# Transposing the experts' activations: TensorE with an identity, or VectorE in blocks of 32 with the blocks exchanged by the loads

## The chip, the cores and the metric

The kernel runs on one core of one Trainium2 chip. The metric is the time of one execution on the device in microseconds (us); lower is better. Three executions of the kernel before took 3319.48 to 3320.54 us, with a median of 3319.95 us.

## The reference, cut to what matters

The model is two transformer-like blocks over 256 tokens of width 2048. The change lies wholly in the last part of the first block, a retrieval over 16,384 experts of one neuron each:

```python
def peer_ffn(h, w_q, sub_keys, u, v):
    ...
    s1, i1 = lax.top_k(scores[:, :, 0], PEER_TOPK)        # 16 of 128 first keys
    s2, i2 = lax.top_k(scores[:, :, 1], PEER_TOPK)        # 16 of 128 second keys
    ...
    cand_idx = i1 * PEER_N_KEYS + i2                      # expert = 128 * first key + second key
    top_scores, top_pos = lax.top_k(cand_scores, PEER_TOPK)
    gates = jax.nn.softmax(top_scores, axis=-1)
    ...
        a = jnp.einsum('td,thkd->thk', xb, u[eb])
        w = gb * jax.nn.gelu(a, approximate=False)
        return jnp.einsum('thk,thkd->td', w, v[eb])
```

The kernel does not gather rows of u and v. It computes gelu(x u^T) for all 16,384 experts as a dense product, multiplies it by a table of gates that is zero wherever a token did not choose an expert, and multiplies the result by v as a second dense product.

## The kernel before

All dense products have one form. `jobs` is a list of 1 MB weight blocks in the order in which they are used; `load` fetches each block into a `raw` tile from SyncE's queue, four blocks ahead. `convert` cuts a block into four pieces of 128x512, and `split` makes of each piece a `hi` part (ScalarE, L208) and a `lo` part (VectorE, L209), so that TensorE works at its fast number format with three matmuls for each 128x512 piece and token block (`passes`, L260, L261, L263). With two token blocks a piece is six matmuls and a job is 24. VectorE and ScalarE prepare up to `PIECES = 7` pieces ahead of TensorE, in eight `hi` and eight `lo` buffers. Work that is not a dense product is put into `tasks`, whose steps are woven in between the pieces: `tasks.step()` runs once for each piece and issues one step for each lane. Every engine runs its instructions in the order in which the program issues them.

The experts' part has two phases:

- The in phase, `expert_in_jobs(g)` for g = 0 to 31: four jobs for each group of 512 experts (four first keys times 128 second keys). At the end of a group `post` applies the gelu on ScalarE (L936) and leaves `ga`, with tokens on partitions and experts along the row. The second product needs experts on partitions. So `work` has TensorE transpose the eight 128x128 blocks against the identity (`transposed`, L230), ScalarE copies the results out of PSUM into `aT` (L942), and GpSimd's queue stores `aT` in device memory as `ad` (L944). This work starts four steps after the group ends.
- The out phase, `expert_out_jobs(pair)` for 16 pairs of groups: eight jobs for each pair. While one pair is multiplied, the next is prepared: before the pair's first and second job `weights_load` issues the loads of one group each, one load of `ad` (L952) and four loads of the gate table (L954), all on GpSimd's queue; before the fourth and the sixth job `weigh` multiplies activations and gates on VectorE (L963) and splits the product into `h` and `l` with one ScalarE and one VectorE instruction of 128x1024 (L208, L209). These are what TensorE loads as weights in the next pair.

During the first half of the in phase VectorE also does the routing (`top`, `route`), and GpSimd scatters the gates into the tables `gd` with 256 indirect DMAs (L914). There is one table for each 64 tokens (`QT = 64`), with second keys along partitions, then first keys, then tokens. SyncE's queue clears the tables beforehand with 16 transfers (L926).

Of the kernel before, what the change touches and what calls it, by code (L numbers as in the profile page):

```python
# [17 lines left out]
F32 = mybir.dt.float32  # L18
# [5 lines left out]
OP = mybir.AluOpType  # L24
AX = mybir.AxisListType

P, T, D, TB = 128, 256, 2048, 2
NEG = -1.0e30
PACE = 3.7
QT = 64  # L30
# [80 lines left out]
def hybrid_block_kernel(ctx: ExitStack, tc: tile.TileContext, a: dict, out: bass.AP):  # L111
    nc = tc.nc
    V, A, G, PE = nc.vector, nc.scalar, nc.gpsimd, nc.tensor
# [9 lines left out]
    dram = ctx.enter_context(tc.tile_pool(name="dram", bufs=1, space=bass.MemoryType.DRAM))  # L123
# [4 lines left out]
    def nm(s):  # L128
        count[0] += 1
        return f"{s}_{count[0]}"  # L130

    def s4(shape, dt=F32):
        return s4p.tile([P] + shape, dt, tag="s4", name=nm("s4"))

    def s2(shape, dt=F32):
        return s2p.tile([P] + shape, dt, tag="s2", name=nm("s2"))

    def small(n):
        t = smp.tile([P, 32], F32, tag="sm", name=nm("sm"))
        return t[:, 0:n]  # L140

    def kept(shape, dt=F32, name="kept", p=P):

        if name in SHARED:
            return const.tile([p] + shape, dt, name=nm(name), tag=SHARED[name], bufs=2)
        return const.tile([p] + shape, dt, name=nm(name))
# [4 lines left out]
    def side():  # L151
        return sidep.tile([P, 512], F32, tag="side", name=nm("side"))
# [53 lines left out]
    def split(hi, lo, src):  # L206

        A.copy(out=hi, in_=src)  # L208
        V.tensor_tensor(out=lo, in0=src, in1=hi.bitcast(F32), op=OP.subtract)  # L209
# [13 lines left out]
    def transposed(src_of, n):  # L223

        for c in range(0, n, 2):
            pt = side()
            pv = pt.rearrange("p (c t) -> p c t", c=2)
            for i in range(min(2, n - c)):
                for tb in range(TB):
                    PE.transpose(pv[:, i, tb * P:(tb + 1) * P], src_of(c + i, tb), ident)  # L230
            yield pv, c
# [17 lines left out]
    tasks = Tasks(4, 4)  # L249
# [53 lines left out]
    S = {}  # L303
# [459 lines left out]
    fox_group(3)  # L763
    out_jobs("f", 1)
    jobs[-4].pre = lambda: S.update(clear_t=tasks.add(clear_tables(), apart=8, lane=1))
    mla_group(3)
    gate_jobs("m", 2)
# [32 lines left out]
    def rf(tb):  # L800
        return S["rf"][:, tb:tb + 1]
# [19 lines left out]
    def peer_q_jobs():  # L821
# [5 lines left out]
        for b in range(4):  # L827
            def post(ps, b=b):
# [32 lines left out]
                for tb in range(TB):  # L861
                    ts = [tasks.add(top(tb, hh), [t], 1, 2) for hh in range(2)]
                    rs.append(tasks.add(route(tb, b), ts, 1, 2))
                S["gates_t"].append(tasks.add(scatter(b), rs + [S["clear_t"]], 1, 3))
            block_jobs([a["wpq"][b, k] for k in range(4)], post, pre=peer_pace if b == 0 else None)

    def route(tb, b):

        hs = slice(2 * b, 2 * b + 2)
        tv, tp, ti = S["tv"][tb][:, hs], S["tp"][tb][:, hs], S["ti"][tb][:, :, hs]  # L870
        pick = S["pick"][tb]
        gp = s2([2, 2, 16])
        gate, place = gp[:, 0], gp[:, 1]
        ab = s2([2, 2, 16], U32)
        V.tensor_tensor(out=gate, in0=tv, in1=tv[:, :, 0:1].to_broadcast([P, 2, 16]), op=OP.subtract)
        V.tensor_scalar(out=ab[:, 0], in0=tp, scalar1=4, scalar2=None, op0=OP.logical_shift_right)
        V.tensor_scalar(out=ab[:, 1], in0=tp, scalar1=15, scalar2=None, op0=OP.bitwise_and)
        A.activation(out=gate, in_=gate, func=AF.Exp)
        abf, ie = s2([2, 2, 16]), s2([2, 2, 16])
        V.tensor_copy(out=abf, in_=ab)  # L880
        yield
        sm, rs = small(2), small(2)
        V.tensor_reduce(out=sm, in_=gate, axis=AX.X, op=OP.add)
        V.reciprocal(out=rs, in_=sm)
        V.tensor_tensor(out=gate, in0=gate, in1=rs[:, :, None].to_broadcast([P, 2, 16]), op=OP.mult)
        for i in range(2):
            eq = s2([2, 16, 16])
            V.tensor_tensor(out=eq, in0=abf[:, i][:, :, :, None].to_broadcast([P, 2, 16, 16]),
                            in1=S["iota"][:, None, None, 0:16].to_broadcast([P, 2, 16, 16]), op=OP.is_equal)
            V.tensor_tensor(out=eq, in0=eq, in1=ti[:, i][:, :, None, :].to_broadcast([P, 2, 16, 16]), op=OP.mult)  # L890
            V.tensor_reduce(out=ie[:, i], in_=eq, axis=AX.X, op=OP.add)
            yield
        V.scalar_tensor_tensor(out=abf[:, 0], in0=ie[:, 0], scalar=float(QT),
                               in1=S["lane"][:, None, :].to_broadcast([P, 2, 16]), op0=OP.mult, op1=OP.add)
        V.scalar_tensor_tensor(out=place, in0=ie[:, 1], scalar=float(P * QT), in1=abf[:, 0], op0=OP.mult, op1=OP.add)
        for to in range(2):
            for half in range(2):
                dst = pick[half * QT:(half + 1) * QT, to, :, hs]
                rows, ks = slice(to * QT, (to + 1) * QT), slice(8 * half, 8 * half + 8)
                V.tensor_copy(out=dst[:, 0], in_=gate[rows, :, ks])  # L900
                V.tensor_copy(out=dst[:, 1].bitcast(U32), in_=place[rows, :, ks])
        yield END

    def scatter(b):

        for h in (2 * b, 2 * b + 1):  # L910
            for k in range(8):
                for q, gd in enumerate(S["gd"]):
                    pick = S["pick"][q // 2][:, q % 2]
                    G.indirect_dma_start(  # L914
                        out=gd.rearrange("p (n o) -> (p n) o", o=1),
                        out_offset=bass.IndirectOffsetOnAxis(ap=pick[:, 1, h, k:k + 1].bitcast(U32), axis=0),
                        in_=pick[:, 0, h, k:k + 1], in_offset=None, compute_op=OP.add)
                yield
        yield END

    def clear_tables():

        S["gd"] = [dram.tile([P, P * QT], F32, name=f"gd{q}") for q in range(T // QT)]
        for i in range(4):
            for gd in S["gd"]:
                nc.sync.dma_start(out=gd[:, i * 2048:(i + 1) * 2048].rearrange("p (a b) -> p a b", a=8),  # L926
                                  in_=warm.bitcast(F32)[:, None, :].to_broadcast([P, 8, 256]))
                yield
        yield END

    def expert_in_jobs(g):

        def post(ps):
            ga = s4([TB, 512])
            for tb in range(TB):
                A.activation(out=ga[:, tb], in_=ps[tb], func=AF.Gelu, scale=rf(tb))  # L936
            aT = s4([4, T])
            S["ad", g] = dram.tile([P, 4 * T], F32, name=f"ad{g}")

            def work():  # L940
                for pv, c in transposed(lambda c, tb: ga[:, tb, c * P:(c + 1) * P], 4):
                    A.copy(out=aT[:, c:c + 2, :], in_=pv)  # L942
                yield
                G.dma_start(out=S["ad", g], in_=aT.rearrange("p j t -> p (j t)"))  # L944
                yield END
            tasks.add(work())
        block_jobs([a["ut"][g, k] for k in range(4)], post)

    def weights_load(g):
        tasks.flush(S["gates_t"])  # L950
        aT, gg = s4([4, T]), s4([T // QT, 4, QT])
        G.dma_start(out=aT.rearrange("p j t -> p (j t)"), in_=S["ad", g])  # L952
        for q, gd in enumerate(S["gd"]):
            G.dma_start(out=gg[:, q].rearrange("p j t -> p (j t)"), in_=gd[:, g * 4 * QT:(g + 1) * 4 * QT])  # L954
        S["loaded", g] = (aT, gg)

    def weigh(g):

        def work():
            aT, gg = S["loaded", g]  # L960
            h, l = s4([4, T], F32R), s4([4, T], F32R)
            av = aT.rearrange("p j (c t) -> p c j t", t=QT)
            V.tensor_tensor(out=av, in0=av, in1=gg, op=OP.mult)  # L963
            split(h, l, aT)
            S["W", g] = (h, l)
            yield END
        S["W_t", g] = tasks.add(work(), (), 1, 1)
# [33 lines left out]
    def peer_start():  # L1001
        iota, lane = kept([16], name="iota"), kept([16], name="lane")
        for dst, step, mul in ((iota, 1, 0), (lane, 0, 1)):
            G.iota(dst, pattern=[[step, 16]], base=0, channel_multiplier=mul,
                   allow_small_or_imprecise_dtypes=True)
        V.tensor_scalar(out=lane[QT:P], in0=lane[QT:P], scalar1=-float(QT), scalar2=None, op0=OP.add)
        S["iota"], S["lane"] = iota, lane

    for g in range(32):
# [590 lines left out]
```

## Time and profile before

| what | value |
|---|---|
| median of three executions | 3319.95 us (3319.48 to 3320.54) |
| profiled execution: its own time | 3319.21 us |
| profiled execution: span of the trace | 3317.4 us |
| TensorE busy in the span | 3288.9 us (99%) |
| VectorE busy | 2324.9 us (70%) |
| ScalarE busy | 1779.5 us (54%) |
| GpSimd busy | 559.3 us (17%) |
| TensorE's granted clock, mean | 0.997 |
| device memory, mean | 204 GB/s |

The span is what the profiler saw from the first to the last instruction; 1.8 us of the execution's own time lie around it. Busy times of an engine count overlapping instructions once. A matmul's duration in the trace is longer than its distance to the next one, because matmuls are pipelined; what a matmul costs is read from the starts.

### The profile page before, as it was taken

How to read it: one execution, taken by the hardware profiler on the slowest of the kernel's cores; microseconds unless marked ns; L12 is line 12 of the kernel's file. 1: busy time of each engine (PE TensorE's matmuls, PEld its weight loads, DVE VectorE, ACT ScalarE, POOL GpSimd, SP SyncE). 2: the span in 40 equal slices, each digit the busy share in tenths (PEclk: the TensorE clock that was granted, in tenths of full speed). 3: DMA queues.
4: the chain of work that ended last, by engine and by line, in shares of the span. 5: the costliest groups of instructions: out<-in, count | busy, mean ns of one | idle time of the engine just before them, and what ended most of it. 6: DMA issues, size and time to landing. Idle time of an engine off the chain costs nothing.

```text
span 3317.4 us, 43290 instructions
## 1 busy us (share of the span) xinstructions
PE 3288.9 (99%) x15275; PEld 2734.3 (82%) x15276; DVE 2324.9 (70%) x4667; ACT 1779.5 (54%) x3125; POOL 559.3 (17%) x494
## 2 busy tenths in 40 slices
PE   9999999999999999999999999999999999999997
PEld 7888888888888888888888888888888888788886
DVE  6677676776677787444566767767668777778767
ACT  6655555554655655555554444444555454455553
POOL 0000000000008777876111111100000000000001
PEclk9999999999999999999999999999999999999999
DMA  6444555688457777777676666665564445444554
GB/s 244 172 159 159 178 178 184 210 267 272 178 184 208 205 215 208 207 216 205 235 278 242 243 249 235 239 235 211 200 224 168 167 170 199 177 165 165 178 190 140
DMA packets 158362, 676.55 MB, mean 204 GB/s; under 512 B 50465, under 2 KB 67249, under 8 KB 86593
## 3 DMA queue, kind: packets, MB, share of 16 engines
q1 hardware_dynamic: 102416, 613.06, 52.6%
q0 software_dynamic: 55296, 60.45, 7.6%
q8 instruction: 119, 1.95, 0.2%
q14 instruction: 99, 0.80, 0.1%
q10 hardware_dynamic: 432, 0.29, 0.0%
HBM read 635.58 MB, written 38.15 MB: 203 GB/s over the span
## 4 chain that ended last, share of the span: by engine, by line
PE 98%; DVE 2%; issue 0%; ACT 0%; DMA 0%; DVEq 0%; SPq 0%
PE acc L263 30%; PE acc L260 30%; PE acc L261 30%; PE side L230 3%; PE side L576 2%; PE side L542 1%; PE side L552 0%; PE side L553 0%; PE side L551 0%; DVE lo L209 0%; DVE X L1318 0%; PE side L839 0%; DMA X<-in_x_dram 0%; DVE X L1323 0%; DVE lst L1304 0%
## 5 line engine op out<-in xcount | busy, mean ns | idle before, releaser
L209 DVE TENSOR_TENSOR lo<-raw,hi 128x512 fp32r<-128x512 f32 x2244 | 1506.1, 689 | 784.3 <-ACT hi L208 775.9
L208 ACT CAST hi<-raw 128x512 fp32r<-128x512 f32 x2244 | 1369.8, 622 | 1128.7 <-DVE lo L209 610.4
L260 PE MATMUL acc<-hi,xh 128*128 128x512 f32 x2816 | 1122.7, 399 | 2.0 <-ACT xh L1352 0.9
L263 PE MATMUL acc<-hi,xl 128*128 128x512 f32 x2816 | 1098.9, 391 | 2.8 <-DVE xl L209 2.8
L261 PE MATMUL acc<-lo,xh 128*128 128x512 f32 x2816 | 1098.4, 390 | 3.0 <-DVE lo L209 3.0
L260 PE MATMUL acc<-hi,s 128*128 128x512 f32 x1664 | 654.5, 393 | 0.0
L261 PE MATMUL acc<-lo,s 128*128 128x512 f32 x1664 | 647.6, 389 | 0.0
L263 PE MATMUL acc<-hi,s 128*128 128x512 f32 x1664 | 646.1, 389 | 0.0
L263 PEld LDWEIGHTS acc<-hi,xl 128*128 128x128 f32 x2816 | 529.5, 188 | 116.0 <-DVE xl L209 4.1
L261 PEld LDWEIGHTS acc<-lo,xh 128*128 128x128 f32 x2816 | 530.2, 188 | 108.3 <-DVE lo L209 4.6
L260 PEld LDWEIGHTS acc<-hi,xh 128*128 128x128 f32 x2816 | 530.2, 188 | 107.7 <-ACT xh L1352 1.6
L914 POOL DMA_INDIRECT gd<-pick x256 | 426.2, 1665 | 89.6 <-issue 73.6
L263 PEld LDWEIGHTS acc<-hi,s 128*128 128x128 f32 x1664 | 312.4, 188 | 65.4
L261 PEld LDWEIGHTS acc<-lo,s 128*128 128x128 f32 x1664 | 312.6, 188 | 63.3
L260 PEld LDWEIGHTS acc<-hi,s 128*128 128x128 f32 x1664 | 312.6, 188 | 63.1
L1329 POOL TENSOR_TENSOR X<-X,s 128x512 f32<-128x512 f32 x6 | 9.0, 1524 | 874.4 <-ACT X L1328 874.4
L535 ACT ACTIVATE s<-s,sm 128x128 f32<-128x128 f32 (+1 forms) x128 | 57.3, 448 | 123.4 <-DVE sm L533 123.4
L1217 DVE SCALAR_TENSOR_TENSOR s<-s,vec,s 128x256 f32<-128x256 f32 x240 | 115.6, 482 | 4.6
L952 POOL DMA_DIRECT2D s<-ad x32 | 17.1, 534 | 483.1 <-PE acc L263 447.7
L944 POOL DMA_DIRECT2D ad<-s x32 | 26.9, 839 | 406.8 <-ACT s L942 406.8
L230 PEld LDWEIGHTS side<-cst,s 128*128 128x128 f32 x720 | 84.1, 141 | 11.1
L230 PE MATMUL side<-cst,s 128*128 128x128 f32 x720 | 92.6, 272 | 0.0
(257 smaller groups left out, 1699.9 us busy)
## 6 DMA issues: line engine op xcount, KB each, us to landing
raw<-in_ut_dram SPq DMA_DIRECT2D x128, 1024.0 KB, 4.9
raw<-in_pv_dram SPq DMA_DIRECT2D x128, 1024.0 KB, 5.3
raw<-in_w_dram SPq DMA_DIRECT2D x120, 1024.0 KB, 4.8
raw<-in_win_dram SPq DMA_DIRECT2D x87, 1024.0 KB, 5.0
raw<-in_wout_dram SPq DMA_DIRECT2D x32, 1024.0 KB, 5.7
raw<-in_wo_dram SPq DMA_DIRECT2D x32, 1024.0 KB, 4.7
gd<-s SPq DMA_DIRECT2D x16, 1024.0 KB, 9.1
raw<-in_wpq_dram SPq DMA_DIRECT2D x16, 1024.0 KB, 4.7
```

What stands on the lines that cost most here:

```text
L208: A.copy(out=hi, in_=src)
L209: V.tensor_tensor(out=lo, in0=src, in1=hi.bitcast(F32), op=OP.subtract)
L230: PE.transpose(pv[:, i, tb * P:(tb + 1) * P], src_of(c + i, tb), ident)
L260: PE.matmul(ps[tb], lhsT=lh[:, kc, t], rhs=wh, start=start, stop=False)
L261: PE.matmul(ps[tb], lhsT=lh[:, kc, t], rhs=wl, start=False, stop=False)
L263: PE.matmul(ps[tb], lhsT=ll[:, kc, t], rhs=wh, start=False, stop=stop)
L535: A.activation(out=pr[:, c], in_=pr[:, c], func=AF.Exp, bias=nmax[:, i:i + 1], accum_out=sums[:, i:i + 1])
L542: PE.transpose(pt[:, i * P:(i + 1) * P], pr[:, i * P:(i + 1) * P], ident)
L576: PE.matmul(sc[:, o0:o0 + k1], lhsT=q[:, q0:q0 + P], rhs=k[:, 0:k1], start=i == 0, stop=i == len(parts) - 1)
L914: G.indirect_dma_start(out=gd.rearrange("p (n o) -> (p n) o", o=1), out_offset=bass.IndirectOffsetOnAxis(ap=pick[:, 1, h, k:k + 1].bitcast ...
L944: G.dma_start(out=S["ad", g], in_=aT.rearrange("p j t -> p (j t)"))
L1217: V.scalar_tensor_tensor(out=cv[:, c], in0=pad[:, k:k + T], scalar=tapw(k), in1=cv[:, c], op0=OP.mult, op1=OP.add)
```

## The change

The transposes by TensorE and the copies out of PSUM go. VectorE transposes `ga` instead, with one instruction for each token block (128x512), which turns each 32x32 block by itself and leaves the blocks where they are among the partitions. `ad` is stored in that form. The loads put the blocks in place: four loads of `ad`, each into 32 partitions, fetch runs of 512 bytes (128 elements) from all 128 rows. What arrives has tokens in another order along the row (token block, 32 tokens, first key, token), so the gate tables are given the same order: `gd` gets a dimension for the two halves of 64 tokens, the scatter's positions change, and each load of a gate table fetches two runs of 512 bytes for each partition where it fetched one of 1 KB. `weigh` writes `h` and `l` back in the old order, through a rearranged view. The task starts one step after the group ends and goes on at each step, where it waited four.

```diff
-        V.scalar_tensor_tensor(out=abf[:, 0], in0=ie[:, 0], scalar=float(QT),
+        V.scalar_tensor_tensor(out=abf[:, 0], in0=ie[:, 0], scalar=32.0,
...
                     G.indirect_dma_start(
-                        out=gd.rearrange("p (n o) -> (p n) o", o=1),
+                        out=gd.rearrange("p i (n o) -> (p i n) o", o=1),
...
-        S["gd"] = [dram.tile([P, P * QT], F32, name=f"gd{q}") for q in range(T // QT)]
+        S["gd"] = [dram.tile([P, 2, P * 32], F32, name=f"gd{q}") for q in range(T // QT)]
...
-                nc.sync.dma_start(out=gd[:, i * 2048:(i + 1) * 2048].rearrange("p (a b) -> p a b", a=8),
+                nc.sync.dma_start(out=gd[:, i // 2, i % 2 * 2048:(i % 2 + 1) * 2048].rearrange("p (a b) -> p a b", a=8),
...
             for tb in range(TB):
                 A.activation(out=ga[:, tb], in_=ps[tb], func=AF.Gelu, scale=rf(tb))
-            aT = s4([4, T])
-            S["ad", g] = dram.tile([P, 4 * T], F32, name=f"ad{g}")
+            gt = s4([TB, 4, 4, 32])
+            S["ad", g] = dram.tile([P, TB, 4, P], F32, name=f"ad{g}")
 
             def work():
-                for pv, c in transposed(lambda c, tb: ga[:, tb, c * P:(c + 1) * P], 4):
-                    A.copy(out=aT[:, c:c + 2, :], in_=pv)
-                yield
-                G.dma_start(out=S["ad", g], in_=aT.rearrange("p j t -> p (j t)"))
+                for tb in range(TB):
+                    V.transpose(out=gt[:, tb].rearrange("p q b c -> p b q c"), in_=ga[:, tb])
+                    yield
+                G.dma_start(out=S["ad", g], in_=gt.rearrange("p t q b c -> p t q (b c)"))
                 yield END
-            tasks.add(work())
+            tasks.add(work(), (), 1)
...
-        aT, gg = s4([4, T]), s4([T // QT, 4, QT])
-        G.dma_start(out=aT.rearrange("p j t -> p (j t)"), in_=S["ad", g])
+        aT, gg = s4([TB, 4, 4 * 32]), s4([T // QT, 2, 4 * 32])
+        for q in range(4):
+            G.dma_start(out=aT[32 * q:32 * q + 32],
+                        in_=S["ad", g][:, :, q].rearrange("(i r) t x -> r t i x", i=4))
         for q, gd in enumerate(S["gd"]):
-            G.dma_start(out=gg[:, q].rearrange("p j t -> p (j t)"), in_=gd[:, g * 4 * QT:(g + 1) * 4 * QT])
+            G.dma_start(out=gg[:, q], in_=gd[:, :, g * 4 * 32:(g + 1) * 4 * 32])
...
-            av = aT.rearrange("p j (c t) -> p c j t", t=QT)
-            V.tensor_tensor(out=av, in0=av, in1=gg, op=OP.mult)
-            split(h, l, aT)
+            av = aT.rearrange("p t i x -> p (t i x)")
+            V.tensor_tensor(out=av, in0=av, in1=gg.rearrange("p q i x -> p (q i x)"), op=OP.mult)
+            hv, lv = (x.rearrange("p b (g c) -> p g b c", c=32) for x in (h, l))
+            split(hv, lv, aT.rearrange("p t i (b c) -> p (t i) b c", b=4))
...
-        V.tensor_scalar(out=lane[QT:P], in0=lane[QT:P], scalar1=-float(QT), scalar2=None, op0=OP.add)
+        for i in range(1, 4):
+            rows = slice(32 * i, 32 * i + 32)
+            V.tensor_scalar(out=lane[rows], in0=lane[rows], scalar1=float(P * 32 * (i % 2) - 32 * i), scalar2=None,
+                            op0=OP.add)
```

## Rows read from the trace of the kernel before

**Rows 1.** The page, part 1: busy us (share of the span), instructions.

```profile
PE   3288.9 (99%) x15275; PEld 2734.3 (82%) x15276; DVE 2324.9 (70%) x4667; ACT 1779.5 (54%) x3125; POOL 559.3 (17%) x494
```

**Rows 2.** The waits of TensorE, whole span: us in total, times, longest.

```profile
PE acc L261 <- DVE lo L209: 3.0, 2, 2.8
...
PE acc L260 <- ACT hi L208: 0.3, 1, 0.3
```

**Rows 3.** Timeline of TensorE, one group of the in phase: start, us, instruction.

```profile
1315.41 1.04 PE L230 MATMUL side<-cst,s 128*128 128x128 f32 x8
1316.21 0.48 PE L260 MATMUL acc<-hi,xh 128*128 128x512 f32 x1
1316.52 0.40 PE L261 MATMUL acc<-lo,xh 128*128 128x512 f32 x1
1316.75 0.39 PE L263 MATMUL acc<-hi,xl 128*128 128x512 f32 x1
...
1337.84 0.40 PE L263 MATMUL acc<-hi,xl 128*128 128x512 f32 x1
1338.07 1.03 PE L230 MATMUL side<-cst,s 128*128 128x128 f32 x8
```

**Rows 4.** Line 230 in 960 to 1700 us: ns min/median/max, first and last start.

```profile
L230 PE MATMUL side<-cst,s x256: 272/272/273, 975.5 to 1678.7; 128*128 128x128 f32 x128
```

**Rows 5.** Groups by line and shape, VectorE: busy us, mean ns, idle before.

```profile
L209 DVE TENSOR_TENSOR lo<-raw,hi 128x512 fp32r<-128x512 f32 x2240 | 1504.4, 689 | 784.3 <-ACT hi L208 775.9 <-PE acc L263 2.9
...
L1323 DVE SCALAR_TENSOR_TENSOR X<-X,sm,s 128x512 f32<-128x512 f32 x10 | 8.2, 850 | 0.1
```

**Rows 6.** Timeline of ScalarE at the end of a group.

```profile
1628.08 1.37 ACT L936 ACTIVATE s<-acc,rf 128x512 f32<-128x512 f32 x2
1629.35 0.61 ACT L208 CAST hi<-raw 128x512 fp32r<-128x512 f32 x1
```

**Rows 7.** Stretches of 80 us: length, busy PE, PEld, DVE, ACT, POOL, clock, DMA.

```profile
1055.00:1135.00 80.00, 80.00 (x371) 66.58 (x370) 64.06 (x175) 46.83 (x76) 58.71 (x39) 1.00 0.74 208
...
1760.00:1840.00 80.00, 80.00 (x354) 66.28 (x353) 56.25 (x82) 39.54 (x63) 7.93 (x15) 1.00 0.68 242
```

**Rows 8.** Timeline of GpSimd's queue, the first two groups that are loaded.

```profile
1612.52 0.53 POOL L952 DMA_DIRECT2D s<-ad  x1
1613.04 2.13 POOL L954 DMA_DIRECT2D s<-gd  x4
...
1619.25 0.54 POOL L954 DMA_DIRECT2D s<-gd  x1 [2.49 <-DMA s<-ad]
```

**Rows 9.** Timeline of GpSimd's queue, loads of a pair in the out phase.

```profile
1756.62 0.53 POOL L952 DMA_DIRECT2D s<-ad  x1 [35.44 <-PE acc L263]
...
1762.06 0.53 POOL L952 DMA_DIRECT2D s<-ad  x1 [2.80 <-PE acc L263]
```

**Rows 10.** Timeline of VectorE, where the same pair is weighed.

```profile
1779.61 1.22 DVE L963 TENSOR_TENSOR s<-s,s 128x1024 f32<-128x1024 f32 x1
...
1790.54 1.22 DVE L963 TENSOR_TENSOR s<-s,s 128x1024 f32<-128x1024 f32 x1
```

**Rows 11.** DMA queues, 1740 to 1827 us: packets, MB, share of 16 engines.

```profile
q1 hardware_dynamic: 2302, 16.76, 54.7%
q0 software_dynamic: 1344, 4.20, 12.8%
```

**Rows 12.** The same view, 700 to 820 us, while the tables are cleared.

```profile
DMA packets 13875, 34.15 MB, mean 285 GB/s; under 512 B 560, under 2 KB 10800, under 8 KB 11184
...
q1 hardware_dynamic: 13420, 32.48, 79.9%
```

**Rows 13.** The same view, 200 to 320 us, weights alone on this queue.

```profile
q1 hardware_dynamic: 2448, 17.83, 42.3%
```

**Rows 14.** Line 1054, a GpSimd DMA of 256 runs: ns min/median/max.

```profile
L1054 POOL DMA_DIRECT2D skew<-s x6: 709/720/739, 2392.6 to 2421.9; - x6
```

## The prediction

> **What bounds the kernel now.** I read the page's busy times first, then the waits of TensorE, then its timeline around one group of the in phase. TensorE is busy for 3288.9 of 3317.4 us [rows 1]. Over the whole span its waits for other engines and DMAs fall into only eight groups, the largest 3.0 us in total and the smallest 0.3 [rows 2], and not one of them lies in the experts' two phases. In 80 us stretches of these phases TensorE is busy all 80, at a granted clock of 1.00, which is the 2.4 GHz level [rows 7]. So in the stretch of the change the time is the sum of TensorE's instructions. What is taken off TensorE is gained in full as long as no other engine or queue falls behind; what is put on another engine costs nothing until then. The prediction has two halves: what the transposes cost TensorE, and whether VectorE, GpSimd's queue and the DMA engines can carry what they get.
>
> **What TensorE loses.** For each group of 512 experts eight transposes go. Their mean of 272 ns [rows 4] is a duration, not a price: matmuls overlap. The price is read from the starts [rows 3]. Between two clusters of eight transposes lie 96 matmuls. From the third of them (1316.75) to the last (1337.84) there are 93 steps in 21.09 us, so 0.2268 us each. From cluster to cluster it is 1338.07 - 1315.41 = 22.66 us. Take away 96 x 0.2268 = 21.77 and 0.89 us are left for eight transposes, 0.11 us each. This counts the somewhat longer step behind the cluster too (1316.21 to 1316.52 is 0.31, not 0.23). All groups are alike: 256 transposes from 975.5 to 1678.7 us [rows 4], and with 0.80 for the last cluster's length, (1678.7 - 0.8 - 975.5) / 31 = 22.66. So 32 x 0.89 = 28.5 us go. Bounds: the distance from the cluster's start to the next matmul's alone is 0.80, which gives 25.6; the cluster's whole 1.04, as if the next matmul did not overlap it, gives 33.3. I take 28.5, since it comes from the period.
>
> The Trainium skill's page "TensorE: Matmul & The Clock Gate" (Part 4: PE-mode transpose) gives about 275 ns for a transpose within a kernel. The row's 272 ns agrees as a duration; as a price the page's figure would take 256 x 0.275 = 70 us off, and the period of 22.66 us speaks against that.
>
> **What VectorE gets.** Two transposes of 128x512 for each group. The trace has no such instruction. Nearest rows: 689 ns for the 128x512 subtraction, 850 ns for the slowest group of that size [rows 5]. I take 0.69 us, with 0.85 as the upper bound; nothing is the lower one. The tightest stretch is the routing: 64.06 of 80 us busy [rows 7]. It holds 80 / 22.66 = 3.53 groups, so 7.06 transposes add 4.9 us (6.0 at most), 69 or 70 of 80. VectorE would be full at (80 - 64.06) / 7.06 = 2.26 us each.
>
> The transpose waits for the gelu, and queued behind it on VectorE are the `lo` halves that TensorE needs. That wait hides: the next `hi` comes behind both gelus on ScalarE (1628.08 to 1629.35 [rows 6]), so the next `lo` could not start before, and the first transpose fits beside the second gelu. The second transpose is issued one piece later. VectorE runs up to seven pieces ahead of TensorE, each six matmuls or 1.36 us: 9.5 us of cover against about 1.4. If that cover were gone, 64 x 0.69 = 44 us would come onto TensorE's path. VectorE has one piece to deliver in each 1.36 us and needs 0.69, so it recovers 0.67 us a piece.
>
> **Edits that I cost at nothing.** The two PSUM copies for each group leave ScalarE, which nobody waits for. The three instructions on `lane` run once. The clears, the scatter and its positions keep their number, size and queue; only addresses change. The product in `weigh` and its split keep their sizes of 128x1024, read or written in runs of 32; were the split twice as slow on both engines, the 9.5 us would cover it. The store of `ad` comes earlier in the order and moves as many bytes; behind it on GpSimd's queue stand the indirect DMAs of the scatter, whose result is wanted only when the first load comes (1612.52 [rows 8]). It waits for VectorE's second transpose where it waited for ScalarE's copies some pieces later, so it holds them up no more than now.
>
> **The loads of the out phase.** This is the part that could go wrong. For each group GpSimd issues eight DMAs where it issued five, and the DMA engines move 2048 runs of 512 B where they moved 128 of 4 KB and 512 of 1 KB; the bytes stay 1 MB.
>
> Issue: 0.53 us for today's loads [rows 8], 0.72 for a transfer of 256 runs [rows 14], as each new one has. So eight take 4.2 to 5.8 us, where groups are 5.4 us apart (1756.62 to 1762.06 [rows 9]). GpSimd has nothing else to do there.
>
> Landing: today's first load of `ad` was issued at 1612.52, and a later load waited for it until 1619.25, that is 6.7 us [rows 8]. The same row shows that GpSimd waits when too many DMAs are under way. The first group is weighed 1779.61 - 1756.62 = 23.0 us after its first issue, the second 1790.54 - 1756.62 = 33.9 us after that same issue [rows 9, 10]. New: 5.8 us of issue and 6.7 to land make 12.5. If the second group's eight had to wait for the whole first set, they would land at 25 us. Both are in time, with 9.5 us of cover behind.
>
> DMA engines: the clears show the price of small runs. In 700 to 820 us the queue's packets took 0.799 x 120 x 16 = 1534 us of engine time, and 10800 - 560 = 10,240 of them are runs of 1 KB (10.49 MB) [rows 12]. Weights alone cost 0.423 x 120 x 16 / 17.83 = 45.5 us for each MB [rows 13], so the other 22.0 MB took 1001 us, and a run of 1 KB took 533 / 10,240 = 52 ns. A run of 512 B costs at most about that and at least its bytes' share. In 87 us of the out phase (two pairs, four groups) there are 8192 of them, 512 for each engine: 26.6 us at 52 ns, against 11.1 now (12.8% of 87). With the weights' 47.6 us (54.7%) that is 74 of 87 us [rows 11]. The queues fill up at (87 - 47.6) / 512 = 77 ns. Weights are fetched four blocks ahead, so a burst delays no piece that TensorE waits for.
>
> The Trainium skill's page "DMA: Bandwidth & Descriptors" (Specifications) puts the smallest transfer at line rate at 512 B. No row here has runs of just that size; by it the loads would cost the DMA engines no more than now.
>
> **Sum.** Profiled execution 3319.21 us - 28.5 = 3290.7. The median of the runs lies 0.7 us above the profiled one, so 3319.95 - 28.5 = 3291.4 us.
>
> **The rivals.**
> - The loads come late (the one that ends slower). If a run of 512 B cost as much as the software queue's mean packet today, 178 us of engine time / 1344 = 132 ns [rows 11], 512 would take 67.8 us, and with the weights 115 us in 87. Eight such stretches add 8 x 28.4 = 227 us: about 3519. It decides from 77 ns a run. For it speaks that no row has bulk runs below 1 KB; against it that a run of 1 KB costs 52, and that the packets of 132 ns average 3 KB. Chance 4%.
> - VectorE's transposes land on TensorE's path in the routing stretch alone, some 14 groups: 14 x 1.38 = 19.3 us given back, 3310.7 us. For it: VectorE is 80% busy there and works in bursts. Against: 9.5 us of cover. Chance 4%. In all 32 groups it would be 44 us: 3335.4, slower. Chance 2%.
> - The transposes were worth their full durations: 256 x 0.272 = 69.6 us less, 3250.4 us. The period of 22.66 us speaks against it. Chance 1%.
> - The change does less than it says, because TensorE only waits in place of transposing, for something that the transposes cover today: 3319.95. No wait in these phases is seen today, and `raw`, `hi` and `lo` are all ahead. Chance 2%.
>
> **How the numbers follow.** The forecast has 87%, with bounds of 25.6 and 33.3 us on the saving, so 3286.7 to 3294.4; with about 1 us for the spread of runs, 3286 to 3296. This alone is over 8 in 10, so it is the range. A measurement of this kernel tells 0.2% (6.6 us) from no change. Faster: forecast 87, the routing case 4, full durations 1: 92%. Within 0.2%: 2%. Slower: 4 and 2: 6%.
>
> **What would show each step.** Line 230 has 256 matmuls fewer; clusters are gone from the in phase, and a group's period falls from 22.66 to 21.77 us. VectorE has 64 new instructions of about 0.69 us, and its busy share in the routing stretch is about 86%. TensorE still waits for nobody in either phase. In the out phase a pair still takes 8 x 24 x 0.2268 = 43.5 us, eight loads a group are issued in 4.2 to 5.8 us, and the software queue's share lies between 13% and 31%. I am wrong if TensorE's waits show `lo` from VectorE in the in phase, or the weighed `h` and `l` in the out phase.

## The result and the profile after

The changed kernel takes 3291.12 us (six runs, 3290.49 to 3291.69) against 3320.24 us for the kernel before in the same comparison: a ratio of 0.9913, 95% interval 0.99 to 0.9925. That is 29.1 us less; 28.5 were forecast. The two profiled executions are 3319.21 and 3291.13 us, 28.1 apart.

TensorE loses 256 matmuls and 30.5 us of busy time, VectorE gains 66 instructions, GpSimd 96. The page's busy line answers to [rows 1]:

```profile
PE 3258.4 (99%) x15019; PEld 2706.2 (82%) x15020; DVE 2360.8 (72%) x4733; ACT 1748.4 (53%) x3061; POOL 644.8 (20%) x590
```

TensorE's timeline in the same part of the in phase as [rows 3]. No cluster stands between the groups any more:

```profile
1315.68 0.39 PE L260 MATMUL acc<-hi,xh 128*128 128x512 f32 x1
1315.91 0.39 PE L261 MATMUL acc<-lo,xh 128*128 128x512 f32 x1
...
1336.76 0.39 PE L260 MATMUL acc<-hi,xh 128*128 128x512 f32 x1
```

From the first row to the last there are 93 steps in 21.08 us, 0.2267 each, the same step as before. A group is 96 such steps, 21.76 us, in place of 22.66. The waits of TensorE, whole span, answer to [rows 2]; the two largest are

```profile
PE acc L261 <- DVE lo L209: 4.9, 4, 2.9
PE acc L263 <- DVE xl L209: 2.8, 1, 2.8
```

and for 940 to 2360 us, which holds both phases, the view has no row. The out phase is as long as it was. The additions of its results to X are L977 before and L984 after; here are their ns min/median/max, first and last start, in the kernel before and then in the changed one:

```profile
L977 DVE TENSOR_TENSOR X<-X,acc x128: 679/682/684, 1685.8 to 2374.5; 128x512 f32<-128x512 f32 x128
```

```profile
L984 DVE TENSOR_TENSOR X<-X,acc x128: 679/681/686, 1657.8 to 2346.6; 128x512 f32<-128x512 f32 x128
```

688.7 and 688.8 us from first to last. The first comes 28.0 us earlier, so the whole gain has arisen by the end of the in phase. VectorE's new instruction, by line and shape (busy us, mean ns, idle before):

```profile
L946 DVE STREAM_TRANSPOSE s<-s 128x512 f32<-128x512 f32 x64 | 45.2, 707 | 6.9 <-ACT s L940 2.6 <-issue 2.0 <-DMA gd<-pick 1.3
```

It costs 0.707 us, and waits 2.6 us in all for the gelu: the wait in VectorE's order is nearly always over when VectorE gets there. The stretches of [rows 7]:

```profile
1055.00:1135.00 80.00, 80.00 (x354) 66.28 (x353) 70.31 (x187) 45.48 (x72) 64.46 (x42) 1.00 0.79 218
...
1760.00:1840.00 80.00, 80.00 (x355) 66.26 (x354) 54.78 (x80) 38.40 (x62) 20.74 (x32) 1.00 0.81 250
```

VectorE is busy for 70.3 of 80 us in the routing stretch, and TensorE for all 80. In the out phase, GpSimd's queue for a pair, which answers to [rows 9], and the DMA queues in 1740 to 1827 us, which answer to [rows 11]:

```profile
1728.68 2.42 POOL L957 DMA_DIRECT2D s<-ad  x4 [29.29 <-DVE lo L209]
1730.99 2.83 POOL L960 DMA_DIRECT2D s<-gd  x4
1734.12 1.21 POOL L957 DMA_DIRECT2D s<-ad  x2 [0.29 <-PE acc L263]
1737.49 0.59 POOL L957 DMA_DIRECT2D s<-ad  x1 [2.16 <-DMA s<-ad]
...
1739.95 2.83 POOL L960 DMA_DIRECT2D s<-gd  x4 [0.40 <-PE acc L263]
```

```profile
q1 hardware_dynamic: 2305, 16.79, 58.8%
q0 software_dynamic: 1491, 4.07, 18.2%
```

The first group's eight loads are issued in 5.1 us (1728.68 to 1733.82). Those of the second group take 8.7 us (1734.12 to 1742.78), since GpSimd waits in between for earlier loads to land, 2.16 us at the longest.

### The profile page after: what moved, and what is told of

The parts are those of the page before. It is cut to its first block, busy times and chain, and to the rows that moved or that the text cites. A ratio compares the mean times of both kernels' runs of the same rounds, so it can differ in the third digit from the quotient of the medians.

```text
span 3289.3 us, 42994 instructions
## 1 busy us (share of the span) xinstructions
PE 3258.4 (99%) x15019; PEld 2706.2 (82%) x15020; DVE 2360.8 (72%) x4733; ACT 1748.4 (53%) x3061; POOL 644.8 (20%) x590
## 4 chain that ended last, share of the span: by engine, by line
PE 98%; DVE 1%; ACT 0%; issue 0%; DMA 0%; DVEq 0%; SPq 0%; ACTq 0%
PE acc L263 31%; PE acc L260 31%; PE acc L261 31%; PE side L230 2%; PE side L576 2%; PE side L542 1%; PE side L552 0%; PE side L553 0%; PE side L551 0%; DVE lo L209 0%; PE side L839 0%; DVE X L1328 0%; DMA X<-in_x_dram 0%; DVE lst L1314 0%; DVE X L295 0%
## 5 line engine op out<-in xcount | busy, mean ns | idle before, releaser
L957 POOL DMA_DIRECT2D s<-ad x128 | 77.1, 622 | 407.2 <-PE acc L263 189.2
L960 POOL DMA_DIRECT2D s<-gd x128 | 90.5, 713 | 19.1 <-DMA s<-gd 7.7
L984 DVE TENSOR_TENSOR X<-X,acc 128x512 f32<-128x512 f32 x128 | 81.9, 681 | 0.0
```

The source lines that it names most:

```text
L957: G.dma_start(out=aT[32 * q:32 * q + 32], in_=S["ad", g][:, :, q].rearrange("(i r) t x -> r t i x", i=4))
L960: G.dma_start(out=gg[:, q], in_=gd[:, :, g * 4 * 32:(g + 1) * 4 * 32])
L984: V.tensor_tensor(out=X[:, tb, c], in0=X[:, tb, c], in1=ps[tb], op=OP.add)
```

## The experiments

### Is it TensorE's transposes?

Eight transposes for each group are put back on TensorE, at their old place. Nothing reads them, and the copies out of PSUM stay away. A second kernel puts back sixteen (`range(2)`).

```diff
             tasks.add(work(), (), 1)
+            def extra():
+                for _ in range(1):
+                    for pv, c in transposed(lambda c, tb: ga[:, tb, c * P:(c + 1) * P], 4):
+                        pass
+                yield END
+            tasks.add(extra())
```

> The changed kernel with eight 128x128 transposes of each group put back on TensorE, four steps after the group's end as before; their result is not read, and the PSUM copies stay away. Theory (the time is TensorE's own sum, 0.89 us for eight transposes): 3291.1 + 32 x 0.89 = 3319.6 us. Rival (the gain comes from ScalarE's lost copies, the free PSUM or the earlier task): clearly less, under 3310 us.

> The same with sixteen transposes for each group. Theory: twice the step, 3291.1 + 57.0 = 3348.1 us. Rival (transposes cost their duration of 0.272 us): 512 x 0.272 = 139 us more, 3430 us. Rival (PSUM buffers of the side tiles make TensorE wait): well over 3348 us, and TensorE's waits name them.

Measured: 3319.71 us with eight (ratio to before 0.9999, 0.9989 to 1.0009) and 3347.21 us with sixteen: steps of 28.6 and 27.5 us, 0.89 and 0.86 for each eight. Between 960 and 2375 us the view of TensorE's waits has no row in either. The timeline with sixteen:

```profile
1351.94 1.91 PE L230 MATMUL side<-cst,s 128*128 128x128 f32 x16
1353.60 0.48 PE L260 MATMUL acc<-hi,xh 128*128 128x512 f32 x1
```

The cluster pushes the next matmul back by 1.66 us, where the cluster of eight takes 0.80 [rows 3]: some 0.10 us a transpose, not the 0.27 of its duration. The eight transposes alone bring back the whole gain, so ScalarE's lost copies and the earlier task have no share in it that the runs could tell. The PSUM buffers come back with the transposes, so this run does not separate them; but TensorE waits for nothing there in either kernel.

### Do the loads or the timing matter by themselves?

In the kernel before, only the loads get the new shape; what arrives has the wrong order, so this kernel's output isn't the reference's. In the changed kernel, only the task's timing goes back (`tasks.add(work())`).

```diff
-        G.dma_start(out=aT.rearrange("p j t -> p (j t)"), in_=S["ad", g])
+        av = aT.rearrange("p j t -> p (j t)").rearrange("p (t i x) -> p t i x", t=TB, i=4)
+        sv = S["ad", g].rearrange("p (t q x) -> p t q x", t=TB, q=4)
+        for q in range(4):
+            G.dma_start(out=av[32 * q:32 * q + 32], in_=sv[:, :, q].rearrange("(i r) t x -> r t i x", i=4))
...
-            G.dma_start(out=gg[:, q].rearrange("p j t -> p (j t)"), in_=gd[:, g * 4 * QT:(g + 1) * 4 * QT])
+            G.dma_start(out=gg[:, q].rearrange("p j t -> p (j t)").rearrange("p (i x) -> p i x", i=2),
+                        in_=gd.rearrange("p (i x) -> p i x", i=2)[:, :, g * 4 * 32:(g + 1) * 4 * 32])
```

> The kernel before with TensorE's transposes kept, and only the loads of the out phase in the new shape: eight DMAs for each group, in runs of 512 bytes. The activations and gates arrive in an order that does not fit, so the output is not the reference's; the work is the same. Theory (loads hidden): 3320 us, within 2 us of before. Rival (the loads come late): slower by 10 us or more. Rival (part of the gain comes from the loads): faster.

> The changed kernel with the task's old timing: it starts four steps after the group's end, and its steps lie four apart. Theory (the timing is worth nothing, VectorE has the cover): 3291 us, within 2 us. Rival (the early start gives part of the gain, or the wait for the gelu costs some): a difference of 3 us or more to either side.

Measured: 3320.41 us (1.0001, 0.9992 to 1.0011) and 3291.24 us (0.9912, 0.9896 to 0.9929). Both are as the theory had it: neither edit moves the time.

### How much cover has VectorE?

Each transpose is issued three or five times; shown is three.

```diff
                 for tb in range(TB):
-                    V.transpose(out=gt[:, tb].rearrange("p q b c -> p b q c"), in_=ga[:, tb])
+                    for _ in range(3):
+                        V.transpose(out=gt[:, tb].rearrange("p q b c -> p b q c"), in_=ga[:, tb])
                     yield
```

> The changed kernel with each VectorE transpose issued three times, 2.1 us for a token block. Theory (VectorE is hidden until it is full, at 2.26 us a token block in the routing stretch, and has 9.5 us of cover): VectorE at 98 to 99% of that stretch, 3291 to 3296 us. Rival (what is added to VectorE lands on TensorE's path): 128 x 0.707 = 90 us more, 3382 us.

> Each VectorE transpose issued five times, 3.5 us for a token block. Theory (VectorE full in the routing stretch alone, some 14 groups): 14 x 2 x (3.5 - 2.26) = 35 us more less the cover, 3310 to 3330 us, and TensorE's waits lie only between about 975 and 1330 us. Rival (on the path everywhere): 256 x 0.707 = 181 us more, 3472 us. Rival (VectorE never matters): 3291 us.

Measured: 3295.79 us with three, 3341.07 with five. With three, 90 us of added VectorE work cost 4.7 us. With five, 181 us cost 50.0, above the 19 to 39 that I had expected. The stretches of the kernel with five (length, busy PE, PEld, DVE, ACT, POOL, clock, DMA):

```profile
1055.00:1135.00 80.00, 72.39 (x299) 57.38 (x298) 76.06 (x190) 36.83 (x59) 56.88 (x37) 0.96 0.68 193
1135.00:1215.00 80.00, 71.75 (x303) 56.99 (x302) 77.22 (x191) 34.82 (x58) 49.80 (x34) 0.98 0.66 180
...
1375.00:1455.00 80.00, 80.00 (x355) 66.24 (x354) 63.01 (x96) 40.56 (x65) 66.64 (x44) 1.00 0.81 225
```

The place is as expected: TensorE waits in the routing stretch and nowhere behind it. Two things were mis-sized. VectorE is full at some 77 of 80 us, not at 80; with three it stands at 76.2 to 77.1 already, and TensorE idles for 1.8 us in the same stretches. And a wait costs more than itself. TensorE's timeline in that kernel:

```profile
1106.26 0.39 PE L260 MATMUL acc<-hi,xh 128*128 128x512 f32 x1
1109.15 0.50 PE L261 MATMUL acc<-lo,xh 128*128 128x512 f32 x1 [2.51 <-DVE lo L209]
...
1110.68 0.63 PE L260 MATMUL acc<-hi,xh 128*128 128x512 f32 x1
1111.11 0.63 PE L261 MATMUL acc<-lo,xh 128*128 128x512 f32 x1
```

Soon after the wait the steps are 0.43 us in place of 0.23: the granted clock has dropped from its 2.4 GHz level to that of 1.2 (it is 0.50 in 1110.2 to 1113.0 us). In 975 to 1375 us TensorE idles for 33.4 us; the granted clock of 0.96 to 0.98 in the same five stretches is worth 80 x (0.02 + 0.04 + 0.02 + 0.02 + 0.02) = 9.6 more, by estimate. Together that is 43 of the 49.4 us between the two profiled executions; the rest stays open.

### How near is the edge of the DMA engines?

All eight loads of a group (2 to 31) are issued a second or a third time, into memory that is free in the out phase; nothing reads it. Shown is the second time.

```diff
+        if g == 2:
+            S["spare"] = [res.tile([P, 2, 2, 1024], F32, tag=t, name=nm(t)) for t in ("xh", "xl")]
+        for k in range(1 if g > 1 else 0):
+            s = (1 * g + k) % 4
+            to = S["spare"][s // 2][:, s % 2]
+            ax, gx = (to[:, j].rearrange("p (t i x) -> p t i x", t=2, i=4) for j in range(2))
+            for q in range(4):
+                G.dma_start(out=ax[32 * q:32 * q + 32],
+                            in_=S["ad", g][:, :, q].rearrange("(i r) t x -> r t i x", i=4))
+            for q, gd in enumerate(S["gd"]):
+                G.dma_start(out=to[:, 1, q * 256:(q + 1) * 256].rearrange("p (i x) -> p i x", i=2),
+                            in_=gd[:, :, g * 4 * 32:(g + 1) * 4 * 32])
```

> The changed kernel with all eight loads of a group issued a second time into memory that is free in the out phase (groups 2 to 31); nothing reads it. The software queue's share in 1740 to 1827 us was 18.2% beside 58.8% for the weights. Theory (hidden while the DMA engines are not full): some 36% and 59%, 95% in all, 3291 to 3294 us. Rival (the loads are at the edge): slower by 10 us or more, and TensorE or VectorE waits for a load.

> All eight loads issued three times. Theory (engine time adds up as the shares say): 55% and 55 to 59% make 109 to 113%, so the out phase gets longer by 9 to 13% of its 650 us, 58 to 85 us, 3350 to 3376 us, with waits for weights. Rival (only bytes count, 11.1 us of engine time in 87 for one set): 47.6 + 33.3 = 81 of 87 us, still hidden, 3291 to 3295 us.

Measured: 3295.21 us with two (four runs: two at 3291, two at 3299) and 3448.89 us with three. The software queue with two sets, 1740 to 1827 us:

```profile
q1 hardware_dynamic: 2364, 17.25, 59.7%
q0 software_dynamic: 3044, 8.31, 38.2%
```

That is 98% of the engines' time, and the edge: the profiled execution, at 3291.3 us, has no wait of TensorE beyond the usual, while two others lose 8 us. Neither the theory nor the rival had that, and what the two wait for is not shown, since neither was profiled. Three sets are past the edge, and by more than I had expected, 158 us against 58 to 85. TensorE's waits and two stretches with three sets:

```profile
PE acc L260 <- ACT hi L208: 106.5, 15, 10.4
PE acc L261 <- DVE lo L209: 11.1, 17, 2.8
```

```profile
1760.00:1840.00 80.00, 71.87 (x305) 58.29 (x304) 41.67 (x61) 28.99 (x47) 44.38 (x69) 0.94 0.98 284
1840.00:1920.00 80.00, 65.02 (x259) 52.35 (x260) 46.39 (x68) 32.40 (x53) 49.20 (x76) 0.87 0.93 262
```

TensorE waits for `hi` and `lo`, which stand behind products that wait for their loads on VectorE. These waits are some 114 us more than usual, over what engine time alone had given. I suppose that GpSimd's order adds to it, since each real load stands behind the copies of the group before; that was not tried by itself. With the rest goes a granted clock of 0.87 to 0.94 in these stretches. The loads also lose their lead over the products: the last load of `ad` is issued 68.2 us before the last product starts in the changed kernel (2216.6 and 2284.8 us), 17.4 us before it with two sets and 13.3 with three. The rival that only bytes count falls.

### When do the loads land?

Each group is weighed right behind its loads, in the changed kernel and in the kernel before.

```diff
-                jobs[at + i].pre = lambda g=g: weights_load(g)
-                jobs[at + 3 + 2 * i].pre = lambda g=g: weigh(g)
+                jobs[at + i].pre = lambda g=g: (weights_load(g), weigh(g))
```

> The changed kernel with each group weighed right behind its loads, three and four jobs earlier, so that VectorE comes to the product about 23.0 - 16.3 = 6.7 us after the first load is issued. Theory (the first group has landed some 12.5 us after its first issue): VectorE waits about 6 us in each pair, the 9.5 us of cover hold, 3291 to 3294 us. Rival (the loads need nearly all of the 23 us that they have): a wait of 13 us and more, 4 us or more for each of 15 pairs on TensorE's path, over 3350 us.

> The kernel before with the same edit. Theory (its five loads land 6.7 to 9 us after the first issue): VectorE waits 0 to 3 us in a pair, 3320 us within 2 us, and the difference of the two waits is what the new loads take longer, about 4 to 6 us. Rival (the new loads are no later than the old ones): the same wait in both kernels.

Measured: 3306.6 us for the changed kernel, 15.5 more than without the edit, and 3320.65 us for the kernel before (1.0001). My theory had 3291 to 3294 for the changed kernel and fails here; so does the rival, which had a loss in each of 15 pairs. Both went by a lead of some 7 us of the loads over the product. In the pairs the lead is far longer: the last load of `ad` is issued at 2230.6 us, and the last product starts at 2276.7. VectorE waits for loads only twice, 9.0 and 8.4 us, at the border of the two phases, and in the kernel before not at all. GpSimd's queue and VectorE there:

```profile
1605.10 0.57 POOL L948 DMA_DIRECT2D ad<-s  x1 [12.95 <-DVE s L946]
1605.66 1.25 POOL L957 DMA_DIRECT2D s<-ad  x2
...
1611.85 0.71 POOL L960 DMA_DIRECT2D s<-gd  x1 [0.87 <-DMA ad<-s]
```

```profile
1619.65 1.23 DVE L969 TENSOR_TENSOR s<-s,s 128x1024 f32<-128x1024 f32 x1 [9.00 <-DMA s<-gd]
```

The loads of group 1 come late because they stand behind the store of `ad` of a late group, and this store waits 12.95 us for VectorE's transposes. The change brought that about: the task now starts one step after its group, so its store gets into GpSimd's order ahead of the loads; in the kernel before, those loads are out before the store. TensorE idles 8.4 us behind the two waits, and its granted clock is 0.83 in two stretches of 20 us, of which this is one:

```profile
1620.00:1640.00 20.00, 16.93 (x65) 13.47 (x66) 14.38 (x22) 12.69 (x21) 5.01 (x8) 0.83 0.57 199
```

A last kernel joins this edit with the task's old timing, so that the store stands behind the loads again.

> The changed kernel weighed at once, as before, and with the task's old timing (four steps apart), so that the store of a late group stands behind the loads of groups 1 and 2 on GpSimd's queue and not ahead of them. Theory (weighing at once cost 15.5 us because VectorE waited 9.0 and 8.4 us for two loads that queued behind stores, which in turn wait for VectorE's transposes, and because TensorE's clock fell behind these waits): both waits go, 3291 to 3294 us. Rival (the loads of 512-byte runs are themselves too late for it): the waits stay, about 3306 us.

Measured: 3291.46 us. The two waits are down to 7.6 us together, 4.0 at most, which the cover hides:

```profile
DVE s L969 <- DMA s<-gd: 7.6, 2, 4.0
```

So the loss came from the order of the queue and not from the shape of the loads. In the kernel weighed at once, from the last load's end of issue to the product that waits for it there are 1619.65 - 1612.56 = 7.1 us, so the estimate of 6.7 to land was about right.

## Why the prediction was right

- **What TensorE loses.** 28.5 us were forecast from the period; the runs give 29.1 and the profiles 28.1, and two doses put back give 28.6 and 27.5. Both bounds were wide enough; the period was the right source, and the duration of 272 ns [rows 4] would have given 70. On this the Trainium skill's page "TensorE: Matmul & The Clock Gate" (Part 4: PE-mode transpose) has about 275 ns, stated for bf16, and the duration here is 272; but that is no price beside other matmuls: sixteen transposes cost 1.66 us. One small misreading: the waits of TensorE before fall into nine groups, the smallest 0.2 us, not into eight; none lies in the two phases.
- **What VectorE gets.** 0.69 us was taken from the 128x512 subtraction; 0.707 came. 69 or 70 of 80 us were forecast in the routing stretch; 70.3 came. That it is hidden is shown with three times the work, which costs 4.7 us where 90 were added; VectorE is full a little earlier than I had put it.
- **Edits costed at nothing.** The timing of the task is worth nothing by itself. But the prediction looked only at the scatter behind the moved store on GpSimd's queue, not at the loads of groups 1 to 3, which fell behind the stores of the last groups. It costs nothing here because the products come late enough: group 1's loads are issued from 1606.93 us, and its product starts at 1632.04.
- **The lead of the loads.** Here the prediction drew a right conclusion from a wrong reading. It took the loads at 1756.62 us for those of the group weighed at 1779.61, and so a lead of 23.0 us. But loads and products come once for each group, both in the order of the groups, 32 of each (here those of the kernel before):

```profile
L952 POOL DMA_DIRECT2D s<-ad x32: 532/533/536, 1612.5 to 2240.8; - x32
L963 DVE TENSOR_TENSOR s<-s,s x32: 1218/1219/1221, 1647.2 to 2312.8; 128x1024 f32<-128x1024 f32 x32
```

The last product starts 72.0 us after the last load of `ad`. Counted through, the product at 1779.61 is the seventh, and its load was issued at 1713.10; the load at 1756.62 is the ninth. So GpSimd runs one pair further ahead than the prediction had it, with 66.5 and 72.0 us for the two groups of a pair in place of 23.0 and 33.9. In the changed kernel the load at 1728.68 has 66.5 us too; the shortest leads are at the border of the phases, 25.1 us for groups 1 and 3. That the error lay on the safe side was luck.

- **The price of the loads.** Issue in 4.2 to 5.8 us was forecast; 5.1 came for the first group of a pair, and 8.7 with waits for the second. A share between 13% and 31% was forecast; 18.2% came. The full queue was put at 77 ns a run; 18.2% of 87 us is 31 ns for each of 512 runs, so two sets of loads just fit and three don't. The 52 ns for a run of 1 KB came from the hardware queue, where each such run is a packet of its own [rows 12]; on GpSimd's queue the packets are of another form (last section). On the kernel before the new loads alone raise the share from 12.8% to 19.7%:

```profile
q1 hardware_dynamic: 2302, 16.76, 57.8%
q0 software_dynamic: 1536, 4.20, 19.7%
```

The packets of the weights, which are the same, take longer too, 57.8% in place of 54.7%; so the time of packets seems to hold some waiting as well, and the shares are no pure cost of the loads.

The Trainium skill's page "DMA: Bandwidth & Descriptors" (Specifications) puts the smallest transfer at line rate at 512 B; the same bytes in such runs took half as much engine time again, so the measurement does not bear it out in full.

- **The rivals.** None took place. Loads that come late and VectorE on TensorE's path were both made to happen by tripling and by five times the work, so they are real limits, a factor of two and of three away.

## What to carry to other kernels

Where one engine never waits, a change that takes work off it gains that work's share of the period, read from the starts of its instructions with and without it; durations of pipelined instructions do not give it. For the engine that takes the work over, count what it can bear in its tightest stretch, and take a few per cent off. How far a queue runs ahead is read by counting loads and uses from the first on, not from the two that stand nearest to each other. When a task is moved to an earlier step, look at every instruction that now stands behind it on its queues, loads of the next phase too.

## What the runs showed of the hardware

- On GpSimd's queue the profile counts packets of some 4 KB, whatever the runs. The packets of all queues, 1740 to 1827 us, for the kernel before and then with the new loads alone:

```profile
DMA packets 3652, 21.03 MB, mean 242 GB/s; under 512 B 576, under 2 KB 576, under 8 KB 1600
```

```profile
DMA packets 3843, 21.02 MB, mean 242 GB/s; under 512 B 768, under 2 KB 768, under 8 KB 1792
```

Between 512 B and 8 KB there are 1024 packets in both, though the runs went from 128 of 4 KB and 512 of 1 KB to 2048 of 512 B for each group. That is 256 for each group's 1 MB, so runs are put together. On the hardware queue the clears' 1 KB runs in [rows 12] are packets of their own, 10,240 of them. What grows with the new loads is the time that the packets take, and the packets under 512 B by 192, 16 for each of the 12 DMAs more.
- A wait of 2.51 us in TensorE, behind one of 0.79 us some 4 us earlier, was followed by steps of 0.43 us in place of 0.23 at a granted clock of 0.50. In two experiments the profiled execution grew by 1.5 times (49.4 / 33.4) and 1.6 times (13.1 / 8.4) of what TensorE idled.
